# Retention head norm: squares folded over 64 partitions, one product with ones in place of two

## The chip, the cores and the metric

The kernel runs on one core of a Trainium2 chip. The metric is the device time of one execution in microseconds (us); the time of a kernel is the median over its runs. Five engines work side by side and meet through semaphores: TensorE (PE in the profile, with PEld for its weight loads), VectorE (DVE), ScalarE (ACT), GpSimd (POOL) and SyncE (SP), which issues most of the transfers.

## The reference, cut to what matters

Two decoder layers over 512 tokens of width 1024, in float32. Layer 0 is a forgetting attention, layer 1 a retention with 12 heads of 128 channels. The change is in the norm at the end of each retention head:

```
def retention(q, k, v):
    ...
    out = out.transpose(1, 0, 3, 2, 4).reshape(B, S, H, dv)
    out = out * lax.rsqrt(jnp.mean(out * out, axis=-1, keepdims=True) + EPS)
    return out.reshape(B, S, H * dv).astype(q.dtype)
...
main = retention(q, k, v)
memo = mem_cross_attention(q_mem, mem_n, w_mem_kv[i])
o = jnp.concatenate([main, memo], axis=-1) * jax.nn.silu(z)
x = x + o @ w_out[i]
```

For each token and head, the 128 squared channels of the head are averaged, and the head is scaled by the inverse root.

## The kernel before, in words

Everything is computed transposed: a head's output `o` is a PSUM tile with its 128 channels on the partitions and the 512 tokens along the free axis. A sum over channels is then a sum over partitions, and TensorE takes it with a product whose stationary operand is `ones` (128x128 of ones): each partition of the result `sb` holds the sum for each token.

TensorE works with operands in a float32 form of fewer bits (fp32r), so each float32 operand is split in two parts: H is the value rounded (an ACT copy into an fp32r tile) and L is what is left (a DVE subtraction). `split_to`, `split_new` and `prep_piece` do this for activations and for weights. A product of two split operands takes three matmuls (`split3`); with `ones`, which is exact, it takes two.

The program is a list of cycles. Each has fillers (projections in pieces of weights: `f_v`, `f_z`, `f_rot`, `f_out`), which keep TensorE busy, and jobs (`g_mem`, `g_fox`, `g_ret`), which are generators whose steps are put between the fillers at offsets from a table. The order on TensorE is exactly the order in which this is written. On the other engines a scheduler sets the order from priorities when the program is built, and it is fixed from then on: each engine takes its instructions one after the other. Tiles come from small rotating pools: two tiles for `s` (the PSUM tiles of the scores, and of `sb` too), two for `p`, five for `dd`, two for `sqs`, four for the weight parts `wH` and `wL`.

`g_ret` is the job of one retention head. Four steps compute scores and split them into `pTH` and `pTL`; two steps (`pv`) multiply them with the values into `o`; at the end of the second, ACT squares `o` (L599) and the square is split (`sqs`, L151 on ACT and L152 on DVE). The next step is the product with ones (`mm_group`, L60), from which ACT and DVE work out the inverse root (L605 to L609), and the last step multiplies it into the gated head (L612 to L616). Twelve heads run this, in pairs; head 0 to head 11 below is their order in time. For the last pair the inverse root is on the way to the output projection that ends the program (`f_out_last`).

When a piece of weights has been used, `retire` calls `prep_piece`, which splits the next raw piece (`wH` on ACT at L130, `wL` on DVE at L131) into the tiles of the pool, and so waits until the matmuls that read these tiles before are done.

Of the kernel before, what the change touches and what calls it, by code (L numbers as in the profile page):

```python
# [8 lines left out]
F32 = mybir.dt.float32  # L9
F32R = mybir.dt.float32r  # L10
I32 = mybir.dt.int32
AF = mybir.ActivationFunctionType
ALU = mybir.AluOpType
# [23 lines left out]
def tile_hybrid(ctx, tc, x_in, mem_in, memT_in, g_cols, norm_g, fin_g, b_f, wv0, wp, index, consts, cosT, sinT, dec, out):  # L37
    nc = tc.nc
    P = 128
# [11 lines left out]
    def ps_at(kind, shape, dt, name):  # L51
        tag = TAGS[kind]
        return psum.tile(shape, dt, name=name, tag=tag, bufs=BUFS[tag])

    V, A, G, PE = nc.vector, nc.scalar, nc.gpsimd, nc.tensor

    def mm_group(ps, terms):
        n = len(terms)
        for i, (l, r) in enumerate(terms):
            PE.matmul(ps, lhsT=l, rhs=r, start=(i == 0), stop=(i == n - 1))  # L60
# [14 lines left out]
    def tile_(tag, shape, dt=F32):  # L75
        return work.tile(shape, dt, name=tag, bufs=BUFS[tag])
# [72 lines left out]
    def split_to(dH, dL, src, scale=None):  # L149
        if scale is None:  # L150
            A.copy(out=dH, in_=src)  # L151
            V.tensor_tensor(out=dL, in0=src, in1=dH.bitcast(F32), op=ALU.subtract)  # L152
        else:
            A.activation(dH, src, AF.Copy, scale=scale)
            V.scalar_tensor_tensor(out=dL, in0=src, scalar=scale, in1=dH.bitcast(F32), op0=ALU.mult, op1=ALU.subtract)

    def split_new(tag, src, scale=None):
        H, L = tile_(tag, [P, 512], F32R), tile_(tag, [P, 512], F32R)
        split_to(H, L, src, scale)
        return H, L  # L160
# [289 lines left out]
    def pt_tiles():  # L450
        return [work.tile([P, 1664], F32R, name=n, bufs=BUFS["pT"]) for n in ("pTH", "pTL")]
# [55 lines left out]
    def pv(o, v, u, pH, pL, js):  # L507
        vH, vL = v
        for j in js:
            c = slice(PTB[j] + j * P, PTB[j] + S)  # L510
            for i, (a, b) in enumerate(split3(vH[:, j, u * P:(u + 1) * P], vL[:, j, u * P:(u + 1) * P], pH[:, c], pL[:, c])):
                PE.matmul(o[:, j * P:], lhsT=a, rhs=b, start=(j == 0 and i == 0), stop=(j == NT - 1 and i == 2))  # L512
# [60 lines left out]
    def g_ret(l, h):  # L573
        pr, u = h // 2, h % 2
        dtab = tile_("cbc", [P, 512])
        nc.sync.dma_start(out=dtab, in_=dec[h])
        pH, pL = pt_tiles()

        def score(j):
            qH, qL = st[l, "q", h]  # L580
            k = st[l, "k", h][:, j * P:(j + 1) * P]
            n = S - j * P
            s = ps_at("s", [P, 512], F32, name="s")
            mm_group(s[:, :n], [(k, qH[:, j * P:]), (k, qL[:, j * P:])])
            p = tile_("p", [P, 512])
            V.tensor_tensor(out=p[:, :n], in0=s[:, :n], in1=dtab[:, :n], op=ALU.mult)  # L586
            c = slice(PTB[j] + j * P, PTB[j] + S)
            split_to(pH[:, c], pL[:, c], p[:, :n])

        for j in range(NT):  # L590
            score(j)
            yield
        o = ps_at("o", [P, 512], F32, name="o")
        v = st[l, "v", pr]
        pv(o, v, u, pH, pL, (0, 1))
        yield
        pv(o, v, u, pH, pL, (2, 3))
        sq = tile_("p", [P, 512])
        A.activation(sq, o, AF.Square)  # L599
        sH, sL = split_new("sqs", sq)  # L600
        yield
        sb = ps_at("s", [P, 512], F32, name="s")
        mm_group(sb, [(ones, sH), (ones, sL)])
        y, t = tile_("dd", [P, 512]), tile_("dd", [P, 512])
        A.activation(y, sb, AF.Abs_reciprocal_sqrt, bias=eps_t, scale=1.0 / 128)  # L605
        A.activation(t, y, AF.Square)
        V.scalar_tensor_tensor(out=t, in0=sb, scalar=128 * EPS, in1=t, op0=ALU.add, op1=ALU.mult)
        if pr < 5:
            V.scalar_tensor_tensor(out=y, in0=t, scalar=-384.0, in1=y, op0=ALU.add, op1=ALU.mult)  # L609
        yield  # L610
        sz = st[l, "z", h]
        V.scalar_tensor_tensor(out=sz, in0=o, scalar=-0.25 / 128, in1=sz, op0=ALU.mult, op1=ALU.mult)  # L612
        V.tensor_tensor(out=sz, in0=sz, in1=y, op=ALU.mult)
        if pr == 5:
            V.scalar_tensor_tensor(out=sz, in0=t, scalar=-384.0, in1=sz, op0=ALU.add, op1=ALU.mult)
        st[l, "g", h] = split_new("gg", sz)  # L616
        yield

    def g_forget():
# [46 lines left out]
        xload=(0, 1, 2, 3, 4),  # L666
    )
    GEN = dict(mem=g_mem, fox=g_fox, ret=g_ret, ret2=g_ret, forget=g_forget, norm=norm_gen, memr=lambda: memr_gen(), xload=lambda: xload_gen())

    cycles = []  # L670
# [45 lines left out]
    def build_layer(l):  # L716
# [11 lines left out]
        for pr in range(6):  # L728
# [30 lines left out]
          start="l1", mode=4)  # L759
# [101 lines left out]
    ones = cst.tile([P, P], F32R, name="ones")  # L861
# [96 lines left out]
```

## Time and profile before

| | |
|---|---|
| median of 3 runs | 941.47 us (941.02 to 941.47) |
| the profiled execution's own time | 941.57 us |
| its span, first to last instruction | 939.8 us |
| mean granted TensorE clock | 0.995 |
| PE busy | 924.9 us, 98% of the span |
| DVE busy | 591.8 us, 63% |
| ACT busy | 436.1 us, 46% |

Times in the rows below are in us from the start of the span of the profiled execution, which took 941.57 us in all. An engine's busy time counts instructions, and matmuls overlap each other, so the distance between the starts of two matmuls is what one costs. In a timeline, a number in square brackets at a row's end is the idle time of the engine before it, with what ended it; rows of several equal instructions show their count as x2.

### The profile page before, as it was taken

The numbers are of one execution on the slowest core, as the hardware profiler recorded it, in microseconds if no ns is written. First come the engines' busy times: TensorE is split into PE (matmuls) and PEld (weight loads), VectorE is DVE, ScalarE is ACT, GpSimd is POOL, SyncE is SP. The second block draws the span as 40 slices with busy tenths as digits, with TensorE's granted clock in tenths as the row PEclk, the third lists the DMA queues.
The fourth block names the chain that finished last, engine by engine and source line by source line (L and its number), as shares of the span: only waits on it lengthen the run. The fifth ranks groups of instructions, "written<-read, shape, count | busy, mean of one in ns | idle before, by whom it ended". The sixth has DMA issues, their size and how long they took to land.

```text
span 939.8 us, 13062 instructions
## 1 busy us (share of the span) xinstructions
PE 924.9 (98%) x5005; PEld 800.0 (85%) x5005; DVE 591.8 (63%) x1041; ACT 436.1 (46%) x747; POOL 34.1 (4%) x92
## 2 busy tenths in 40 slices
PE   8999999999999999999999999999999999999995
PEld 6988888889888889898898888888889888888984
DVE  5766564555645545655457856667767575856876
ACT  6654453433433324433334435546356454745564
POOL 0200100000000000000000100000000000000001
PEclk9999999999999999999999999999999999999998
DMA  8863332222323213222332152322342234333202
GB/s 290 334 216 111 109 108 89 82 86 79 114 68 102 93 59 118 84 96 68 103 101 90 45 177 71 90 90 79 101 132 74 93 107 122 103 101 105 89 21 90
DMA packets 32486, 100.74 MB, mean 107 GB/s; under 512 B 4380, under 2 KB 4636, under 8 KB 32424
## 3 DMA queue, kind: packets, MB, share of 16 engines
q1 hardware_dynamic: 30840, 96.76, 31.7%
q0 software_dynamic: 864, 2.10, 0.7%
q10 hardware_dynamic: 720, 1.05, 0.3%
q8 instruction: 39, 0.64, 0.3%
q14 instruction: 23, 0.19, 0.1%
HBM read 92.53 MB, written 4.22 MB: 103 GB/s over the span
## 4 chain that ended last, share of the span: by engine, by line
PE 95%; ACT 1%; DVE 1%; POOL 1%; issue 1%; DMA 0%; POOLq 0%; ACTq 0%; DVEq 0%
PE acc L220 44%; PE acc L60 32%; PE s L60 6%; PE o L512 5%; PE acc L408 3%; PE pt L546 1%; PE o L60 1%; PE pt L481 1%; PE acc L353 1%; PE acc L347 1%; PE pt L196 1%; ACT dd L772 0%; DMA vv<-in_memT_dram 0%; DVE wL L131 0%; POOL rstd L188 0%
## 5 line engine op out<-in xcount | busy, mean ns | idle before, releaser
L131 DVE TENSOR_TENSOR wL<-raw,wH 128x1024 fp32r<-128x1024 f32 x148 | 180.9, 1223 | 133.3 <-ACT wH L130 75.6
L130 ACT CAST wH<-raw 128x1024 fp32r<-128x1024 f32 x148 | 154.8, 1051 | 100.3 <-PE acc L220 53.7
L220 PE MATMUL acc<-hL,wH 128*128 128x512 f32 x608 | 162.8, 394 | 0.0
L220 PE MATMUL acc<-hH,wH 128*128 128x512 f32 x608 | 153.5, 394 | 0.0
L220 PE MATMUL acc<-hH,wL 128*128 128x512 f32 x608 | 150.6, 390 | 0.0
L60 PE MATMUL acc<-wH,gg 128*128 128x512 f32 x448 | 146.1, 393 | 0.0
L220 PEld LDWEIGHTS acc<-hH,wL 128*128 128x128 f32 x608 | 114.1, 188 | 24.4
L220 PEld LDWEIGHTS acc<-hH,wH 128*128 128x128 f32 x608 | 111.1, 188 | 21.2
L220 PEld LDWEIGHTS acc<-hL,wH 128*128 128x128 f32 x608 | 111.3, 188 | 20.7
L60 PE MATMUL acc<-wH,hH 128*128 128x256 f32 (+1 forms) x384 | 109.4, 285 | 0.0
L60 PE MATMUL acc<-wH,hL 128*128 128x256 f32 (+1 forms) x384 | 108.7, 283 | 0.0
L60 PE MATMUL acc<-wL,hH 128*128 128x256 f32 (+1 forms) x384 | 108.6, 283 | 0.0
L60 PEld LDWEIGHTS acc<-wH,gg 128*128 128x128 f32 x448 | 84.2, 188 | 17.0
L60 PE MATMUL acc<-wL,gg 128*128 128x512 f32 x224 | 87.3, 390 | 0.0
L310 DVE TENSOR_TENSOR x<-acc,x 128x512 f32<-128x512 f32 x80 | 54.8, 688 | 40.6 <-PE acc L60 38.5
L60 PEld LDWEIGHTS acc<-wL,hH 128*128 128x128 f32 x384 | 73.4, 191 | 0.4
L60 PEld LDWEIGHTS acc<-wH,hH 128*128 128x128 f32 x384 | 73.3, 191 | 0.5
L60 PEld LDWEIGHTS acc<-wH,hL 128*128 128x128 f32 x384 | 73.3, 191 | 0.0
L536 ACT ACTIVATE p<-dd,nm 128x128 f32<-128x128 f32 (+3 forms) x48 | 27.0, 563 | 66.3 <-DVE nm L532 66.1
L151 ACT CAST pTH<-pt 128x128 fp32r<-128x128 f32 (+2 forms) x64 | 29.7, 467 | 56.6 <-PE pt L546 43.9
L60 PE MATMUL s<-qk 128*128 128x256 f32 (+3 forms) x240 | 54.5, 328 | 0.6 <-DVE p L586 0.6
L151 ACT CAST gg<-sz 128x512 fp32r<-128x512 f32 x32 | 19.9, 621 | 74.7 <-DVE sz L447 31.5
(154 smaller groups left out, 1187.2 us busy)
## 6 DMA issues: line engine op xcount, KB each, us to landing
raw<-in_wp_dram SPq DMA_DIRECT2D x146, 512.0 KB, 3.5
cbc<-c_d SPq DMA_DIRECT2D x12, 256.0 KB, 3.3
cbc<-in_dec_dram SPq DMA_DIRECT2D x12, 256.0 KB, 3.7
dd<-dd SPq DMA_DIRECT2D x48, 64.0 KB, 2.0
x<-in_x_dram SPq DMA_DIRECT2D x4, 512.0 KB, 7.7
raw<-in_wv_dram SPq DMA_DIRECT2D x2, 536.0 KB, 4.1
vv<-in_memT_dram SPq DMA_DIRECT2D x2, 512.0 KB, 4.5
vv<-in_mem_dram SPq DMA_DIRECT2D x2, 512.0 KB, 7.7
```

The source lines that it names most:

```text
L60: PE.matmul(ps, lhsT=l, rhs=r, start=(i == 0), stop=(i == n - 1))
L130: A.copy(out=H[:, :n], in_=raw[:, :n])
L131: V.tensor_tensor(out=L[:, :n], in0=raw[:, :n], in1=H[:, :n].bitcast(F32), op=ALU.subtract)
L151: A.copy(out=dH, in_=src)
L196: PE.transpose(pt[:, k, :], xn[:, c:c + P], ident)
L220: PE.matmul(box["ps"], lhsT=a[:, k * P:(k + 1) * P], rhs=b[:, k, :], start=(n == 0), stop=(n == 23))
L310: V.tensor_tensor(out=dst, in0=ps, in1=dst, op=ALU.add)
L347: PE.matmul(ps, lhsT=a, rhs=b, start=(i == 0), stop=False)
L353: PE.matmul(ps, lhsT=a, rhs=b, start=False, stop=(i == 2))
L408: PE.matmul(box[b], lhsT=a, rhs=w, start=(i == 0 and n == 0), stop=(i == 3 and n == 5))
L512: PE.matmul(o[:, j * P:], lhsT=a, rhs=b, start=(j == 0 and i == 0), stop=(j == NT - 1 and i == 2))
L536: A.activation(p[:, :n], dd[:, :n], AF.Exp, bias=nm, scale=-1.0, accum_out=sm)
```

## The change

The squares are taken in two halves: ACT squares channels 64 to 127 into partitions 0 to 63 of a `dd` tile and channels 0 to 63 into partitions 0 to 63 of the `p` tile, and DVE adds them. The 64 rows are split, with the rounded part in partitions 0 to 63 of one `sqs` tile and the rest in its partitions 64 to 127. One product of that tile with `ones` then sums both parts.

```
-        sq = tile_("p", [P, 512])
-        A.activation(sq, o, AF.Square)
-        sH, sL = split_new("sqs", sq)
+        sq, so = tile_("p", [P, 512]), tile_("sqs", [P, 512], F32R)
+        lo, hi = slice(0, 64), slice(64, 128)
+        s2 = tile_("dd", [P, 512])
+        A.activation(s2[lo, :], o[hi, :], AF.Square)
+        A.activation(sq[lo, :], o[lo, :], AF.Square)
+        V.tensor_tensor(out=sq[lo, :], in0=sq[lo, :], in1=s2[lo, :], op=ALU.add)
+        A.copy(out=so[lo, :], in_=sq[lo, :])
+        V.tensor_tensor(out=so[hi, :], in0=sq[lo, :], in1=so[lo, :].bitcast(F32), op=ALU.subtract)
         yield
         sb = ps_at("s", [P, 512], F32, name="s")
-        mm_group(sb, [(ones, sH), (ones, sL)])
+        PE.matmul(sb, lhsT=ones, rhs=so, start=True, stop=True)
```

In the changed kernel the two squares are L601 and L602, the sum is L603, the copy L604, the subtraction L605 and the product L608; lines behind it are five higher than before (L612 is L617).

The built programs show what stands where. On TensorE nothing moves: at each of the twelve places one matmul stands where two stood. This is the place of head 10, where the product comes right behind the second half of a gate projection (`f_z`, L220) and ahead of the next head's second scores:

```order
 L220 MATMUL acc<-hL,wH 128x512 x4
 L220 MATMUL acc<-hH,wL 128x512 x8
-L60 MATMUL s<-sqs,ones 128x512 x2
+L608 MATMUL s<-sqs,ones 128x512
 L60 MATMUL s<-qk 128x384 x2
 L220 MATMUL acc<-hH,wH 128x512 x8
```

The neighbours of the product are the same in both programs.

On DVE at head 10, before, the subtraction for `sqs` follows the first scores' product with the decay table (L586), ahead of `pTL` and of a piece of weights (`wL`):

```order
L131 TENSOR_TENSOR wL<-raw,wH 128x1024
L586 TENSOR_TENSOR p<-s,cbc 128x512
L152 TENSOR_TENSOR sqs<-p,sqs 128x512
L152 TENSOR_TENSOR pTL<-p,pTH 128x512
L131 TENSOR_TENSOR wL<-raw,wH 128x1024
L586 TENSOR_TENSOR p<-s,cbc 128x384
```

And at the same place on DVE now:

```order
L131 TENSOR_TENSOR wL<-raw,wH 128x1024
L586 TENSOR_TENSOR p<-s,cbc 128x512
L603 TENSOR_TENSOR p<-p,dd 64x512
L152 TENSOR_TENSOR pTL<-p,pTH 128x512
L131 TENSOR_TENSOR wL<-raw,wH 128x1024
L605 TENSOR_TENSOR sqs<-p,sqs 64x512
L236 SCALAR_TENSOR_TENSOR sz<-sz,acc 128x512
```

The sum has taken the old place of the subtraction, and the subtraction now stands behind the piece of weights. On ACT at the same head the copy moves in the same way. This is ACT before, from the square on:

```order
L599 ACTIVATE p<-o 128x512
L151 CAST sqs<-p 128x512
L151 CAST pTH<-p 128x512
L130 CAST wH<-raw 128x1024
L235 ACT_TABLE_LOAD
```

And this is ACT now:

```order
L601 ACTIVATE dd<-o 64x512
L602 ACTIVATE p<-o 64x512
L151 CAST pTH<-p 128x512
L130 CAST wH<-raw 128x1024
L604 CAST sqs<-p 64x512
L235 ACT_TABLE_LOAD
```

The copy for `sqs` now comes behind `pTH` and `wH`.

## Rows read from the trace of the kernel before

**Rows 1.** The page's first part: busy us, share of the span, instructions.
```profile
PE 924.9 (98%) x5005; PEld 800.0 (85%) x5005; DVE 591.8 (63%) x1041; ACT 436.1 (46%) x747; POOL 34.1 (4%) x92
```

**Rows 2.** The instructions on tile sqs: ns min/median/max, first and last start, forms.
```profile
L60 PE MATMUL s<-sqs,ones x24: 388/393/469, 651.9 to 915.4; 128*128 128x512 f32 x24
L151 ACT CAST sqs<-p x12: 615/622/625, 648.0 to 913.3; 128x512 fp32r<-128x512 f32 x12
```

**Rows 3.** Timeline of PE, 17 matmuls of 512 columns apart, nothing between.
```profile
926.22 0.39 PE L347 MATMUL acc<-wH,gg 128*128 128x512 f32 x1
...
930.07 0.39 PE L353 MATMUL acc<-wH,gg 128*128 128x512 f32 x1
```

**Rows 4.** The instructions on tile qk, 640 to 940 us: those over 64 partitions.
```profile
L254 ACT CAST qk<-dd x20: 616/621/623, 643.5 to 873.2; 64x512 fp32r<-64x512 f32 x20
...
L256 DVE TENSOR_TENSOR qk<-dd,qk x10: 684/686/689, 652.5 to 873.9; 64x512 fp32r<-64x512 f32 x10
```

**Rows 5.** Timeline, heads 0 and 4: square and product.
```profile
646.71 0.60 ACT L599 ACTIVATE p<-o 128x512 f32<-128x512 f32 x1
...
651.93 0.62 PE L60 MATMUL s<-sqs,ones 128*128 128x512 f32 x2
...
739.85 0.60 ACT L599 ACTIVATE p<-o 128x512 f32<-128x512 f32 x1 [4.00 <-PE o L512]
...
748.30 0.62 PE L60 MATMUL s<-sqs,ones 128*128 128x512 f32 x2
```

**Rows 6.** Timeline, head 1: subtraction, next scores, product.
```profile
670.92 0.69 DVE L152 TENSOR_TENSOR sqs<-p,sqs 128x512 fp32r<-128x512 f32 x1
...
672.35 1.16 DVE L586 TENSOR_TENSOR p<-s,cbc 128x512 f32<-128x512 f32 x2
...
673.19 0.70 PE L60 MATMUL s<-sqs,ones 128*128 128x512 f32 x2 [0.53 <-DVE p L586]
```

**Rows 7.** Timeline, head 2: square, copy, product, next scores.
```profile
690.41 0.60 ACT L599 ACTIVATE p<-o 128x512 f32<-128x512 f32 x1
691.04 0.62 ACT L151 CAST sqs<-p 128x512 fp32r<-128x512 f32 x1
...
693.42 0.63 PE L60 MATMUL s<-sqs,ones 128*128 128x512 f32 x2
693.62 0.69 DVE L586 TENSOR_TENSOR p<-s,cbc 128x512 f32<-128x512 f32 x1 [1.23 <-PE s L60]
...
694.37 0.62 PE L60 MATMUL s<-qk 128*128 128x384 f32 x2 [0.32 <-DVE p L586]
```

**Rows 8.** Timeline, head 3: subtraction and product.
```profile
713.27 0.69 DVE L152 TENSOR_TENSOR sqs<-p,sqs 128x512 fp32r<-128x512 f32 x1
...
714.19 0.62 PE L60 MATMUL s<-sqs,ones 128*128 128x512 f32 x2
```

**Rows 9.** Timeline, head 10: gate projection, product, piece of weights.
```profile
896.46 2.00 PE L220 MATMUL acc<-hH,wL 128*128 128x512 f32 x8
...
898.29 0.62 PE L60 MATMUL s<-sqs,ones 128*128 128x512 f32 x2
898.55 1.23 DVE L131 TENSOR_TENSOR wL<-raw,wH 128x1024 fp32r<-128x1024 f32 x1 [0.69 <-ACT wH L130]
```

**Rows 10.** Timeline, head 11: square, residual sum, product, last projection.
```profile
912.66 0.60 ACT L599 ACTIVATE p<-o 128x512 f32<-128x512 f32 x1 [5.67 <-PE o L512]
...
914.56 0.68 DVE L310 TENSOR_TENSOR x<-acc,x 128x512 f32<-128x512 f32 x1
...
915.22 0.62 PE L60 MATMUL s<-sqs,ones 128*128 128x512 f32 x2
...
921.05 0.50 PE L353 MATMUL acc<-wH,gg 128*128 128x512 f32 x1 [0.28 <-ACT gg L151]
```

**Rows 11.** Windows: PE, PEld, DVE, ACT, POOL busy (x); clock, DMA share, GB/s.
```profile
5.60:9.00 3.40, 1.55 (x7) 0.73 (x5) 2.21 (x4) 3.39 (x7) 0.00 (x0) 1.00 1.02 408
9.00:12.40 3.40, 3.40 (x8) 2.75 (x9) 3.40 (x6) 3.40 (x7) 0.00 (x0) 0.50 1.03 410
```

## The prediction

> **What bounds the kernel now.** I read the page's busy shares first: PE is busy for 98% of the span, DVE for 63%, ACT for 46% [rows 1]. Then PE's waits in the second layer, where the retention is: in the heads' steps there are three, 0.53 us ahead of head 1's product and 0.32 at heads 2 and 6, each for the product of scores and decay table on DVE [rows 6, 7]. So PE sets the time, and whatever is taken off PE is gained in full, as long as each matmul's operands are there when PE comes to it. The reader should therefore look at two things only: what one matmul costs PE, and how much earlier than PE the squares are ready at each of the twelve places. The timeline around each place answers the second.
>
> **What is removed.** Twelve of the 24 products with ones [rows 2]. The 393 ns there is not the price, since matmuls overlap: where 512-column matmuls follow each other without a wait, 17 steps take 930.07 - 926.22 = 3.85 us, 0.227 us each [rows 3]. If no place is late, 12 x 0.227 = 2.7 us are gained.
> The Trainium skill (TensorE: Matmul & The Clock Gate, section Back-to-back issue gap) gives about 131 ns per 512-column matmul in a sustained stream of loads and matmuls. By that the same twelve would be worth 1.6 us; the trace's 0.227 us is the measurement and decides.
>
> **What is added.** The way from `o` to the product was square, copy, subtraction. It becomes square, square, sum, copy, subtraction, over 64 partitions. The trace has instructions over 64 partitions and 512 columns: an ACT copy takes 0.62 us and a DVE subtraction 0.69 us [rows 4], just what the copy for `sqs` and its subtraction take over 128 [rows 2, 6]. So nothing gets shorter by halving. The two squares cost 0.60 us each, like L599 [rows 5], the sum 0.69, the copy 0.62, the subtraction 0.69. With 0.03 us from one to the next, as from head 2's square to its copy [rows 7], the way takes 0.60 + 0.60 + 0.69 + 0.62 + 0.69 + 4 x 0.03 = 3.3 us instead of 2.0, if neither engine has anything else to do. No transfer is added, and the queue of SP keeps its order. A `dd` tile more per head could make the first square wait for an older tile of that pool; its earlier users are swaps and roots of heads long done, and I cost this at nothing.
>
> **Place by place**, with the product's start in the trace:
>
> *Heads 0, 4, 5, 8, 9.* Head 4's square starts at 739.85 and its product at 748.30 [rows 5]: 8.4 us for a way of 3.3. Heads 5, 8 and 9 have the same pattern and at least as much. Head 0 has 651.93 - 646.71 = 5.2 us [rows 5]; two other DVE instructions come between sum and subtraction there, 1.4 us, and it still holds. Each gains 0.227: 5 x 0.227 = -1.14.
>
> *Head 1.* The subtraction ran from 670.92 to 671.61, then other work, and the scores' product with the table at 672.35; PE waited for that table product, because `sb` takes the tile it frees [rows 6]. Now the sum takes the place at 670.92, the copy runs to 672.26, the subtraction to 672.98, and the table product, which stands behind it on DVE, starts at 672.90 (on DVE an instruction that waits for nothing starts some 0.08 us before the last one's end). PE's product is 0.55 later and one matmul shorter: +0.32.
>
> *Heads 2 and 6.* Square at 690.41, so ready at 690.41 + 3.32 = 693.73 for a product at 693.42 [rows 7]: 0.3 late. But PE waited at 694.37 anyway, for the table product that starts at 693.62, when its scores are done [rows 7]. The subtraction is off DVE in time for that, so PE goes on at 694.37 as before: the lost start and the saved matmul both vanish in that wait. 0.
>
> *Heads 3 and 7.* Here DVE is behind: the subtraction starts at 713.27 only when DVE has come to it, ends at 713.96, and the product follows at 714.19 [rows 8]. Now the sum stands at 713.27, the copy runs from 713.99 to 714.61, the subtraction from 714.64 to 715.33, and the product starts at 715.39 (0.06 from DVE to PE, as at 694.37 [rows 7]): 1.20 late, less 0.227, +0.97. Twice: +1.94.
>
> *Head 10.* DVE has the subtraction behind a piece of weights now. That piece may start only when PE has read the old contents of its tile, and the last matmuls that read them are those right ahead of the product: they start at 896.46, end at 898.46, and the piece started at 898.55, though the ACT copy named beside it was over half a microsecond earlier [rows 9]. It ends at 899.78; the subtraction runs from 899.70 to 900.39, and the product starts at 900.45, not 898.29: 2.16 late, less 0.227, +1.93. This does not depend on how early the squares are: PE itself releases what its next matmul waits for, one 1.23 us instruction and one 0.69 us instruction later.
>
> *Head 11.* Square at 912.66 [rows 10]; the second ends at 913.89, the sum at 914.61, the copy at 915.27. On DVE the residual sum (0.68 us) and the gate's first product (0.69 us) come between, so the subtraction runs from about 915.75 to 916.44 and the product starts at 916.50 for 915.22: 1.28 late, less 0.227, +1.05. The root behind it is on the way to the last projection, which waits for it already [rows 10], so nothing of it is taken back.
>
> **Sum.** -1.14 + 0.32 + 0 + 1.94 + 1.93 + 1.05 = +4.1 us on the profiled execution's 941.57: 945.7. That execution lies 0.1 above the median of the runs, so the forecast is 945.6, slower by 0.44%. Bounds of what the rows don't settle: after a wait, PE may need up to 0.07 more from the first matmul to the next, at five places (the two products of head 1, behind a wait, end 0.70 after their start, those of head 0 0.62 [rows 5, 6]); the second square may start 0.1 us before the first has ended, -0.1 at head 11; DVE's lag at heads 3 and 7 may be 0.4 smaller or 0.1 larger, since it is the end of a long queue. The likeliest case's own range is 944.5 to 946.4.
>
> **Rivals.**
> *The clock falls.* PE would stand still for 2.0 us at head 10. In the trace PE was busy for 1.55 of the 3.40 us from 5.60, and the granted clock of the next 3.40 us was 0.50, the level of 1.2 GHz [rows 11]. If the stop at head 10 did the same, 3.4 us at half speed would cost 1.7: 947.3. For it: PE stood still for 1.85 us in that stretch, no longer than here. Against it: that was in two pauses at the program's start, and around head 10 PE is busy without a gap. 15 in 100. The Trainium skill (TensorE: Matmul & The Clock Gate, section HAM oscillation) warns only of pauses longer than any here, and by that this rival would not come; the rows at 5.60 show a fall without such a pause.
> *Half the partitions, half the time.* If the 64-partition squares and sums took 0.3 to 0.35 us, heads 0, 1, 4, 5, 8 and 9 would gain 0.227 each (-1.36), heads 3 and 7 lose 0.12 each, head 11 0.2 and head 10 still 1.6, because of the piece of weights: +0.7, so 942.1, no difference to speak of. Against it: 0.62 and 0.69 us over 64 partitions [rows 4]. 8 in 100.
> *All hidden.* If ACT and DVE came to each place early enough, the whole -2.7 would be left: 938.8, faster. It decides at head 10: once the piece of weights there runs ahead of the last gate matmuls, or behind the subtraction, 1.9 of the loss goes, and a lead of 1.3 us at heads 3, 7 and 11 takes the rest. Against it: the order on DVE is fixed, and PE itself holds that piece [rows 9]. 4 in 100.
>
> **Chances.** The forecast's case has 73 in 100. A measurement of this kernel tells about 0.2% (1.9 us) from no change, so slower means above 943.35: 0.88 (forecast, clock). Within 0.2%: 0.08. Faster: 0.04. The range leaves out the last two rivals and takes in the clock: 943.2 to 947.5.
>
> **What would show it.** In the changed kernel's profile: PE's waits name DVE `sqs` with 5 to 6 us in all, over seven places; the longest, 2 us, is at head 10, with a piece of weights on DVE just ahead of the subtraction. Heads 0, 4, 5, 8 and 9 show no wait and heads 2 and 6 the old end of theirs. Each new instruction takes 0.6 to 0.7 us. The step that would be wrong if the time stays at 941: that the subtraction at head 10, or DVE at heads 3 and 7, is late as worked out; if it is 947, the clock row around 900 us should be below 1.

## The result, and the profile after

The changed kernel takes 946.6 us (median of 4 runs, 945.5 to 947.7) against 941.47: slower by 0.55%, ratio 1.0055 with a 95% interval of 1.0042 to 1.0068. The forecast was 945.6, slower by 0.44%. The profiled execution of the changed kernel took 946.04 us with a span of 944.3, that of before 941.57 with 939.8.

First the page's busy shares of the changed kernel, in the form of [rows 1]:

```profile
PE 923.5 (98%) x4993; PEld 796.7 (84%) x4993; DVE 600.3 (64%) x1053; ACT 443.1 (47%) x759; POOL 34.3 (4%) x92
```

PE has lost its twelve matmuls (5005 to 4993) and 1.4 us of busy time, and the span is 4.5 us longer. So PE must stand still for longer than before. Where, its waits tell: PE of the changed kernel from 580 to 945 us, with what was waited for, us in total, times, longest.

```profile
PE s L608 <- DVE sqs L605: 5.2, 4, 2.1
PE s L608 <- DVE p L586: 1.2, 1, 1.2
PE s L60 <- DVE p L586: 0.4, 2, 0.2
PE acc L353 <- ACT gg L151: 0.3, 1, 0.3
```

The first row is new: four times PE comes to the product with ones and the subtraction for `sqs` isn't done. The other waits stood there before too, but the one ahead of head 1's product has grown from 0.53 us [rows 6] to 1.2. What the added instructions cost, the groups by tile tell (ns min/median/max, first and last start, forms), of `dd` and of `sqs`:

```profile
L601 ACT ACTIVATE dd<-o x12: 594/595/598, 646.4 to 915.9; 64x512 f32<-64x512 f32 x12
L603 DVE TENSOR_TENSOR p<-p,dd x12: 676/682/684, 647.6 to 917.2; 64x512 f32<-64x512 f32 x12
...
L604 ACT CAST sqs<-p x12: 609/621/627, 648.4 to 917.9; 64x512 fp32r<-64x512 f32 x12
L605 DVE TENSOR_TENSOR sqs<-p,sqs x12: 684/685/685, 649.6 to 919.1; 64x512 fp32r<-64x512 f32 x12
```

The copy over 64 partitions takes 621 ns where the one over 128 took 622 [rows 2]: half the partitions buy nothing.

Then the timeline of the changed kernel at heads 1, 2, 3, 10 and 11 (start, us, engine, line, operation; in brackets the idle time before it and what ended it), to be held against [rows 6 to 10]:

```profile
670.36 0.68 DVE L603 TENSOR_TENSOR p<-p,dd 64x512 f32<-64x512 f32 x1
...
671.72 0.69 DVE L605 TENSOR_TENSOR sqs<-p,sqs 64x512 fp32r<-64x512 f32 x1
672.44 1.16 DVE L586 TENSOR_TENSOR p<-s,cbc 128x512 f32<-128x512 f32 x2
...
673.28 0.47 PE L608 MATMUL s<-sqs,ones 128*128 128x512 f32 x1 [1.18 <-DVE p L586]
...
694.30 0.62 PE L60 MATMUL s<-qk 128*128 128x384 f32 x2 [0.23 <-DVE p L586]
...
713.20 0.68 DVE L603 TENSOR_TENSOR p<-p,dd 64x512 f32<-64x512 f32 x1
...
714.56 0.68 DVE L605 TENSOR_TENSOR sqs<-p,sqs 64x512 fp32r<-64x512 f32 x1
...
715.29 0.51 PE L608 MATMUL s<-sqs,ones 128*128 128x512 f32 x1 [0.97 <-DVE sqs L605]
...
897.68 2.00 PE L220 MATMUL acc<-hH,wL 128*128 128x512 f32 x8
897.69 0.68 DVE L603 TENSOR_TENSOR p<-p,dd 64x512 f32<-64x512 f32 x1
...
899.77 1.23 DVE L131 TENSOR_TENSOR wL<-raw,wH 128x1024 fp32r<-128x1024 f32 x1 [0.69 <-PE acc L220]
...
901.03 0.68 DVE L605 TENSOR_TENSOR sqs<-p,sqs 64x512 fp32r<-64x512 f32 x1
...
901.76 0.50 PE L608 MATMUL s<-sqs,ones 128*128 128x512 f32 x1 [2.09 <-DVE sqs L605]
...
902.10 0.51 PE L60 MATMUL s<-qk 128*128 128x384 f32 x2
...
919.10 0.69 DVE L605 TENSOR_TENSOR sqs<-p,sqs 64x512 fp32r<-64x512 f32 x1
...
919.84 0.50 PE L608 MATMUL s<-sqs,ones 128*128 128x512 f32 x1 [1.12 <-DVE sqs L605]
```

At head 3 the sum stands at 713.20, where the subtraction stood at 713.27 [rows 8], and the subtraction comes 1.36 us later. At head 10 the profile now names PE's own gate matmuls as what released the piece of weights (0.69 us idle ahead of it), and the rows give the whole round: PE's eight matmuls at 897.68, the piece at 899.77, the subtraction at 901.03, the product at 901.76.

What a wait row shows isn't quite what a place costs, since the ends of matmuls are modelled. So I took the same matmul some 30 matmuls behind each product in two profiled executions; how much its distance in time grows from one head to the next is what the head cost (+) or gained (-). The method leaves out what an execution brings along from the program's start. There the changed kernel's clock did not fall, as that of before did [rows 11]; its window reads

```profile
9.00:12.40 3.40, 3.40 (x15) 2.81 (x16) 3.40 (x6) 3.40 (x7) 0.00 (x0) 1.00 1.04 411
```

and it came to the heads 0.33 us ahead. The profiled executions of this document come there anywhere from 0.30 us behind that of before to 0.85 ahead, those with the fall at the start from 0.30 behind to 0.21 ahead, those without it from 0.33 to 0.85 ahead, though the changes touch nothing there. The table is free of this; a measured time holds it.

In the table "addition" is the kernel with the product issued twice (below), "removal" the one that only drops the second product, "moved" the one with the products in later places and nothing folded, "best" the folded one with the later places.

| head | forecast | changed | addition | removal | moved | best |
|---|---|---|---|---|---|---|
| 0 | -0.23 | -0.23 | 0.00 | -0.23 | 0.00 | -0.23 |
| 1 | +0.32 | +0.44 | +0.66 | -0.22 | -0.78 | -1.00 |
| 2 | 0 | +0.09 | +0.07 | +0.03 | -0.58 | -0.84 |
| 3 | +0.97 | +1.02 | +1.44 | -0.21 | 0.00 | -0.23 |
| 4, 5, 8, 9 | -0.91 | -0.91 | 0.00 | -0.91 | 0.00 | -0.90 |
| 6 | 0 | +0.06 | +0.07 | +0.03 | -0.58 | -0.84 |
| 7 | +0.97 | +1.08 | +1.44 | -0.20 | +0.01 | -0.23 |
| 10 | +1.93 | +2.11 | +2.36 | -0.23 | -0.03 | -0.28 |
| 11 | +1.05 | +1.16 | +1.41 | -0.23 | +0.01 | 0.00 |
| sum | +4.1 | +4.8 | +7.45 | -2.17 | -1.95 | -4.55 |

The changed kernel's +4.8 less the 0.33 of the start is the 4.47 between the two profiled executions (946.04 - 941.57).

### The profile page after: what moved, and what is told of

Its sections match the earlier page's. It is cut to its first block, busy times and chain, and to the rows that moved or that the text cites. A ratio compares the mean times of both kernels' runs of the same rounds, so it can differ in the third digit from the quotient of the medians.

```text
span 944.3 us, 13060 instructions
## 1 busy us (share of the span) xinstructions
PE 923.5 (98%) x4993; PEld 796.7 (84%) x4993; DVE 600.3 (64%) x1053; ACT 443.1 (47%) x759; POOL 34.3 (4%) x92
## 3 DMA queue, kind: packets, MB, share of 16 engines
q10 hardware_dynamic: 720, 1.05, 0.3%
## 4 chain that ended last, share of the span: by engine, by line
PE 89%; DVE 5%; ACT 3%; issue 1%; POOL 1%; DMA 0%; POOLq 0%; DVEq 0%; ACTq 0%
PE acc L220 41%; PE acc L60 31%; PE s L60 5%; PE o L512 4%; PE acc L408 2%; PE pt L546 1%; DVE wL L131 1%; PE o L60 1%; PE pt L481 1%; PE acc L353 1%; PE acc L347 1%; PE pt L196 1%; ACT wH L130 1%; DVE p L586 0%; ACT dd L777 0%
## 5 line engine op out<-in xcount | busy, mean ns | idle before, releaser
L220 PE MATMUL acc<-hL,wH 128*128 128x512 f32 x608 | 162.8, 394 | 0.0
L220 PE MATMUL acc<-hH,wH 128*128 128x512 f32 x608 | 153.4, 394 | 0.0
L220 PE MATMUL acc<-hH,wL 128*128 128x512 f32 x608 | 150.6, 390 | 0.0
L220 PEld LDWEIGHTS acc<-hH,wL 128*128 128x128 f32 x608 | 114.1, 188 | 24.4
L220 PEld LDWEIGHTS acc<-hH,wH 128*128 128x128 f32 x608 | 111.0, 188 | 21.2
L220 PEld LDWEIGHTS acc<-hL,wH 128*128 128x128 f32 x608 | 111.3, 188 | 20.6
L310 DVE TENSOR_TENSOR x<-acc,x 128x512 f32<-128x512 f32 x80 | 54.7, 687 | 36.4 <-PE acc L60 34.2
```

The lines of the kernel that those rows point to most:

```text
L220: PE.matmul(box["ps"], lhsT=a[:, k * P:(k + 1) * P], rhs=b[:, k, :], start=(n == 0), stop=(n == 23))
L310: V.tensor_tensor(out=dst, in0=ps, in1=dst, op=ALU.add)
```

## The experiments

The theory: a product with ones is worth 0.227 us of PE, and each of the twelve places where PE comes to the product before the longer chain of squares is done costs its own lateness. The rivals: what is saved is worth less or is lost everywhere; half the partitions take half the time; the clock falls behind the long stop at head 10; DVE as a whole has become the bound.

**The changed kernel again.** No edit.

> The changed kernel as it is, in more executions, since its four so far fall into two pairs: 945.5 and 946.0 at a mean clock of 0.997, 947.2 and 947.7 at 0.995. Late products alone (first theory): one value with a spread of some 0.6 us, as the kernel before shows. Late products, and a fall of the clock in some executions behind the longest stop (second theory): two groups about 1.7 us apart, the slower one always at the lower clock; and if the profiled execution is of the slower group, its clock row around 900 us is below 1.

Measured: 946.5 us (945.69 to 947.47, 5 runs), ratio 1.0056 (1.0043 to 1.0068). Its profiled execution was the longest of the five, 947.47, and shows what the other did not. Its timeline of PE behind the stop:

```profile
901.54 0.67 PE L608 MATMUL s<-sqs,ones 128*128 128x512 f32 x1 [2.09 <-DVE sqs L605]
902.01 0.84 PE L60 MATMUL s<-qk 128*128 128x384 f32 x2
902.65 3.15 PE L220 MATMUL acc<-hH,wH 128*128 128x512 f32 x8
```

And its windows there (busy us of PE, PEld, DVE, ACT and POOL with their counts, granted clock, DMA share, GB/s):

```profile
899.00:902.00 3.00, 0.91 (x4) 0.40 (x3) 2.36 (x3) 2.95 (x5) 0.00 (x0) 0.95 0.00 0
902.00:906.00 4.00, 4.00 (x13) 3.32 (x12) 3.15 (x6) 2.51 (x4) 0.00 (x0) 0.61 0.01 2
906.00:910.00 4.00, 4.00 (x22) 3.34 (x21) 1.71 (x4) 2.06 (x4) 0.00 (x0) 1.00 0.00 0
```

In the changed kernel's first profile the same windows read:

```profile
899.00:902.00 3.00, 0.91 (x4) 0.45 (x4) 2.23 (x4) 2.95 (x5) 0.00 (x0) 1.00 0.00 0
902.00:906.00 4.00, 4.00 (x20) 3.36 (x20) 3.70 (x8) 2.65 (x4) 0.00 (x0) 1.00 0.00 2
```

The same stop of 2.09 us, and once the granted clock behind it is 0.61 on the mean of four microseconds, most of them at 1.2 GHz, once it stays at 2.4. Eight matmuls take 3.15 us instead of 2.00. The place of head 10 costs 3.69 us here instead of 2.11: 1.6 for the clock, close to the rival's 1.7. So this rival is a true part of at least one execution, on top of the forecast's mechanism and not in its place.

That the runs fall into groups doesn't show it by itself. The kernel before does so too: of its 23 runs beside these, 15 took 940.64 to 941.08 us and 8 took 941.73 to 942.09, so the spread of 0.6 us that was expected of a kernel without the stop was too small. With the table's +4.8 and what the program's start brings along, 0.30 behind to 0.85 ahead, an estimate for the changed kernel without a fall at head 10 is 945.5 to 946.7 us. Five of its nine runs lie there. The four from 947.1 to 947.7 lie above; for one of them the profile shows the fall, for the other three it is not shown.

**The removal alone**: the kernel before without its second product (the low parts are left out of the sum of squares).

```diff
-        mm_group(sb, [(ones, sH), (ones, sL)])
+        mm_group(sb, [(ones, sH)])
```

> The kernel before with the product of the low part left out, so that the small part of the squares is not summed; squares and split stay as they were. It is the removal alone, with no longer way to the product. If each product is worth 0.227 us on PE, ten places gain and heads 2 and 6 lose it in their waits: -2.3 us, 939.2. If the way to the product mattered before too, or PE gave the time back later: 941.0 to 941.5. If a product is worth its 0.39 us of the profile: 937.

Measured: 939.33 us (9 runs) for 940.98 of before, ratio 0.9978 (0.9968 to 0.9987). In the table ten heads gain 0.20 to 0.24 each and heads 2 and 6 nothing, as the old wait there takes it back. The term 0.227 stands.

**The addition alone**: the changed kernel with its product issued twice, the second writing over the first.

```diff
         PE.matmul(sb, lhsT=ones, rhs=so, start=True, stop=True)
+        PE.matmul(sb, lhsT=ones, rhs=so, start=True, stop=True)
```

> The changed kernel with its one product with ones issued twice, the second writing over the first: the added vector work alone, with nothing saved on PE. Theory (the saved matmul is worth 0.227 us wherever no later wait takes it back, ten of twelve places): 2.3 us above the changed kernel, so 948.1 where its executions without a fall of the clock lie at 945.8, and up to 949.8 where the clock falls at head 10. Rival (a product is worth 0.13 us): 1.3 above, 947.1. Rival (the saving was lost everywhere, since something else ends each stretch): as the changed kernel, 945.8 to 947.5.

Measured: 949.09 us (4 runs) for 941.15, ratio 1.0082 (1.0068 to 1.0095); 2.6 above the changed kernel's 946.5, or 2.4 with each less its own before; by the table 2.6. The saved matmul is there in full in the changed kernel, behind the late heads as well: 0.22 to 0.25 more at each place but 2 and 6, and 0.42 and 0.36 at heads 3 and 7, 0.3 more than expected in all. What is more than a matmul there comes from heads 2 and 6 and arrives by DVE. Behind the second product of head 2 the root on ACT starts at 694.39 us for 694.12. `pTH` and `pTL` follow it, and DVE, which has one wait from there on, still starts head 3's sum 0.19 later (713.39 for 713.20), while PE's scores ahead of the product start at 713.70 for 713.69. At head 7 the sum is 0.14 later, measured from PE's matmuls. The rival of 0.13 us for a product falls. This execution stopped for 2.1 us at head 10 too, and its clock did not fall.

**The fold everywhere but at head 10.**

```diff
+        fold = h != 10
+        if fold:
...
+        else:
+            sq = tile_("p", [P, 512])
+            A.activation(sq, o, AF.Square)
+            sH, sL = split_new("sqs", sq)
```

> The changed kernel with head 10 alone done in the old way (one square of 128 partitions, two products). First theory, the subtraction behind a piece of weights at head 10: its stop of 2.1 us goes, and the time is 2.1 us below the changed kernel's 945.5 to 946.0, about 943.7; with the clock theory the slower group goes too, and all executions are within some 0.6 us. If the stop at head 10 were only the length of the way, or something that all heads share, less than 1.3 us would go.

Measured: 944.13 us (7 runs) for 940.98, ratio 1.0028 (1.0018 to 1.0039). One head of twelve carries 2.4 of the 5.5 us between 946.5 and 940.98, the fall of the clock included; by the same matmul in the profiled execution its place costs 0.00. The 0.6 us expected for the spread was a miss: the runs span 1.3 (943.44 to 944.77), and those of the kernel before, which has no such stop, span 1.45.

**The fold at heads 0, 4, 5, 8 and 9 alone**: the same edit with `fold = h in (0, 4, 5, 8, 9)`.

> The fold only at heads 0, 4, 5, 8 and 9, whose products come 5 to 9 us behind their squares; the other seven heads in the old way. First theory: no wait at these five, 5 x 0.227 = 1.1 us gained on the kernel before: 940.3. If the longer way, the extra dd tile or the 64-partition instructions cost something at every head, the gain is smaller or gone: 941.0 to 942.

Measured: 939.72 us (11 runs) for 940.98, ratio 0.9985 (0.9976 to 0.9994). Head by head it gains 0.22 to 0.24 five times, 1.14 in all, as the forecast's first term. So the added vector work costs nothing where the squares have time, and DVE and ACT as a whole are not the bound.

**Head 10's product one place later.** A planner step of head 10 is put off, so that PE does the next head's 384-column scores and twelve gate matmuls first; the fold stays.

```diff
-                for off in OFF[kind]:
+                offs = list(OFF[kind])
+                if kind in ("ret", "ret2"):
+                    offs[6] += LATE.get(args[1], 0.0)
+                for off in offs:
```

with `LATE = {10: 0.7}`.

> The changed kernel with head 10's product alone moved 0.7 of a planner step later, which puts it on PE behind the next head's 384-column scores and the next twelve gate matmuls (2.9 us) instead of ahead of them. Theory (the 2.1 us stop is the round of PE's gate matmuls, weights piece on DVE, subtraction, product, and nothing else is late there): the stop goes, the saved matmul shows, 2.1 + 0.2 = 2.3 us below the changed kernel, 943.5 without a fall of the clock, and no execution 1.7 us above the others. Rival (the wait moves to the scores, whose tile the table product on DVE has to free): 0.5 to 1 us of it stays, 944 to 944.5. Rival (the clock falls in any case): executions near 945.2 too.

Measured: 943.88 us (943.16 to 944.4, 8 runs) for 941.15, ratio 1.0028 (1.0017 to 1.0038). Its timeline at head 10:

```profile
899.02 0.51 PE L60 MATMUL s<-qk 128*128 128x384 f32 x2
899.28 1.22 DVE L131 TENSOR_TENSOR wL<-raw,wH 128x1024 fp32r<-128x1024 f32 x1 [0.69 <-PE acc L220]
899.37 2.00 PE L220 MATMUL acc<-hH,wH 128*128 128x512 f32 x8
900.53 0.69 DVE L605 TENSOR_TENSOR sqs<-p,sqs 64x512 fp32r<-64x512 f32 x1
901.20 1.07 PE L220 MATMUL acc<-hL,wH 128*128 128x512 f32 x4
...
902.11 0.40 PE L608 MATMUL s<-sqs,ones 128*128 128x512 f32 x1
```

The piece of weights still waits for PE's gate matmuls and the subtraction still stands behind it, done at 901.22. But PE has twelve matmuls to do meanwhile, and no row of PE has a wait. Head 10 gains 0.28. The scores did not take over the wait, so that rival falls, and the runs span 1.2 us where those of the changed kernel span 2.2.

**Six products later**: the same edit with `LATE = {1: 0.7, 2: 0.7, 3: 0.7, 6: 0.7, 7: 0.7, 10: 0.7}`.

> The changed kernel with the products of heads 1, 2, 3, 6, 7 and 10 moved 0.7 of a planner step later; heads 0, 4, 5, 8, 9 and 11 where they were. Theory (the loss is lateness of the squares at the place where PE comes to them, and nothing else): all but head 11 gain 0.23 each, head 11 loses 1.15 as before: 941.0 - 2.5 + 1.1 = 939.6. Rival (DVE is what is short there, so the root and the gate behind the product wait in place of the product): 0.5 to 1 us of loss per moved head in the next waits of PE, 942 to 945. Rival (the fold costs nothing there and only the order on DVE matters): the same as theory.

Measured: 937.66 us (4 runs) for 941.15, ratio 0.9963 (0.995 to 0.9977). That is 1.9 us better than the theory's 939.6. PE's waits from 580 to 945 us:

```profile
PE s L608 <- DVE sqs L605: 1.1, 1, 1.1
PE acc L353 <- ACT gg L151: 0.3, 1, 0.3
```

Head 11's stop alone is left, and the old waits for the table product (L586), which the kernel before had at heads 1, 2 and 6 [rows 6, 7], are gone as well. I had not counted these.

**The same, and head 11 the old way**: both edits, with `fold = h != 11`.

> As the kernel with six products later, and head 11 alone done the old way (one square over 128 partitions, two products), since nothing stands behind its product that could hide the fold. Theory: eleven matmuls of 0.23 us saved and no wait added, 941.0 - 2.5 = 938.5, 0.27% faster than the kernel before, 1.2 us faster than the one with only five heads folded. Rival (DVE short, later waits): 941 to 944. Rival (the order on DVE moves around head 11 too, a new wait of 0.5 us): 939.0.

Measured: 936.86 us (936.34 to 937.19, 5 runs) for 941.15, ratio 0.9951 (0.9939 to 0.9964): faster than both kernels. One wait of PE is left in these heads:

```profile
PE acc L353 <- ACT gg L151: 0.3, 1, 0.3
```

Expected were 938.5; what the other 1.6 us are, the last run tells.

**The later places without the fold**: the kernel before with the six products later.

> The kernel before, nothing folded, both products of heads 1, 2, 3, 6, 7 and 10 moved 0.7 of a planner step later, as in the kernel with the six moved and head 11 old, which took 936.9. Theory (two gains that add: eleven saved matmuls, 2.5 us, and the three old waits of the kernel before for the table product on DVE, 1.2 us, with what follows a wait, which the later place of the product takes away): 936.9 + 2.5 = 939.4, 1.2 to 1.8 us below the kernel before, and no wait of PE for the table product in the profile. Rival (the old waits went because of the fold, whose shorter turn on PE lets DVE come first): the old waits stay, 941. Rival (everything comes from the new place, and the fold is worth nothing there): 937.

Measured: 939.59 us (11 runs) for 941.36, ratio 0.998 (0.9971 to 0.9989). PE's waits in the same stretch:

```profile
PE acc L353 <- ACT gg L151: 0.3, 1, 0.3
```

The old waits go with the later place alone, worth 0.78 us at head 1 and 0.58 at heads 2 and 6, 1.95 together. From here to the folded kernel it is 936.86 against 939.59, each less its own before: 2.5 us, eleven times 0.227. The two gains add, and both rivals fall.

## Why the prediction was right

*What bounds the kernel; what is removed.* Right. Five heads with time to spare gained 0.22 to 0.24 us each, as forecast; the removal alone and the addition alone give the same size. By the figure of the Trainium skill that the prediction weighed, 131 ns (TensorE: Matmul & The Clock Gate, section Back-to-back issue gap), a place would gain 0.13; the places here gained 0.20 to 0.24, and the measurement decides.

*What is added.* Right: 0.595, 0.682, 0.621 and 0.685 us for square, sum, copy and subtraction, forecast 0.60, 0.69, 0.62 and 0.69. This settles the rival of half the time.

*Head 1.* The mechanism is as forecast, the table product behind the subtraction; +0.44 for +0.32. The 0.1 is an overlap on DVE that didn't come: the table product was to start 0.08 us before the subtraction's end, and it started 0.03 behind it, at 672.44 for an end of 672.41. *Heads 2 and 6.* The saving goes into the old wait for the table product, as forecast: 0.32 us idle before, 0.23 now, +0.09 and +0.06. That it came to 0 was worked out wrongly, though: the subtraction's own end of 693.73 lies behind the table product's 693.62, so it wasn't off DVE in time, and the table product came 0.07 and 0.06 later. *Heads 3 and 7.* +1.02 and +1.08 for +0.97, with the sum in the old place of the subtraction; the product was 1.14 and 1.18 late for 1.20.

*Head 10.* The round from PE's gate matmuls through the piece of weights and the subtraction back to PE came as worked out; the run without the fold there and the run with the product later show that it costs 2.1 and that only PE's coming too early makes it cost anything. It cost 0.18 more than forecast: from the start of the eight matmuls to the product it took 901.76 - 897.68 = 4.08 us for 900.45 - 896.46 = 3.99 forecast, since the subtraction did not overlap here either (the piece ends at 901.00, it starts at 901.03), and from the product to the next matmul 0.34 instead of 0.227. *Head 11.* +1.16 for +1.05, with the same 0.1 behind the wait (919.84 to 920.17).

*The sum* came out at +4.8 for +4.1. Of the 0.7 between them 0.45 is the term set at nothing and named as a bound, the first matmul behind a wait: 0.34 us to the next matmul instead of 0.227 at heads 3, 7, 10 and 11. Head 1, the fifth place of that bound, had its wait before too. The subtraction without overlap at heads 1 and 10 is 0.2, heads 2 and 6 are 0.15, and heads 3 and 7 gave about 0.1 back.

The median of 946.6 lies 1.0 above the forecast and 0.2 above the likeliest case's own range of 944.5 to 946.4; it is inside the whole range because that takes in the clock. The places account for 946.3 (941.47 + 4.8). The remaining 0.3 isn't told apart: the four runs are 945.5, 946.04, 947.16 and 947.7, and the fall at head 10 and the program's start can both move them. The 15 in 100 for the clock were put on the wrong question: the fall is no other case but comes on top in some executions, 1.6 us for the 1.7 worked out, shown in the one of 947.47.

*What would show it.* The total (5.2 us), the longest wait (2.09 at head 10) and the heads without one came as said. Wrong was the count of seven places: four waits name `sqs`, at heads 3, 7, 10 and 11. At heads 1, 2 and 6 the table product is later than the subtraction and is named in its place, as the working itself implied.

## What to carry to other kernels

An engine that is 98% busy gains from a dropped matmul only where its operands are early, so a change that shortens the bound engine and lengthens the chain that feeds it has to be priced place by place; here five places gained 1.1 us and five others lost 5.8. A new instruction pair on a busy engine is not late by its own length but by what already stands between its two halves, and worst where that piece waits for the bound engine itself. Before giving such a change up, move the consumer one unit of work later. With head 11 left the old way, since nothing stands behind its product, that took away the losses and old waits with them, and turned 0.55% slower into 0.49% faster. Of the 0.49%, 0.2% come from the later places alone.

## What the runs showed of the hardware

The clock of TensorE fell behind a single stop of 2.09 us, with PE busy without a gap ahead of it, in one of the three profiled executions that have this stop (the changed kernel's two and that of the addition); it cost 1.6 us. The eight matmuls behind took 3.15 us for 2.00. What tells the executions apart stays open: the stop has the same length in all three. The stops of 0.97 to 1.2 us at heads 1, 3, 7 and 11 went by without a fall in every profile that has them.
The Trainium skill (TensorE: Matmul & The Clock Gate, section HAM oscillation) warns of pauses longer than this one; the execution of 947.47 us differs from that.

On DVE most instructions whose operands are there start some 0.08 us before the last one ends. The subtractions whose result goes to the other half of the partitions do not, and neither does what follows them: all twelve of L605 are followed 0.03 us or more after their end, and all ten of L256 in the kernel before stand 0.03 us from both neighbours, as L256 here, while L586 starts 0.08 before the end of L310:

```profile
651.83 0.69 DVE L152 TENSOR_TENSOR pTL<-p,pTH 128x512 fp32r<-128x512 f32 x1
652.55 0.69 DVE L256 TENSOR_TENSOR qk<-dd,qk 64x512 fp32r<-64x512 f32 x1
653.27 0.69 DVE L310 TENSOR_TENSOR x<-acc,x 128x512 f32<-128x512 f32 x1
653.88 0.55 DVE L586 TENSOR_TENSOR p<-s,cbc 128x384 f32<-128x384 f32 x1
```

It isn't the 64 partitions alone: the sum L603, which stays in its half, is followed 0.07 us before its end at nine places. What in these subtractions does it no run tells apart. The working could have taken this from the trace of the kernel before.

A wait of PE is worth more than its row says. The wait rows of the kernel before at heads 1, 2 and 6 show 0.53, 0.32 and 0.32 us [rows 6, 7]; taking them away gave 0.78, 0.58 and 0.58, about 0.26 more each. The idle time in a row counts from the modelled end of the last matmul: a matmul lasts 0.393 us there [rows 2] where the next can start 0.227 after it [rows 3], which is 0.17 of the 0.26. The first two matmuls behind the wait of head 1 last 0.70 us, for 0.62 elsewhere [rows 5, 6], which is 0.08 more.
